# Column sums, statistics, gates, PSUM banks and weight splits in the first half of a two-layer decoder trunk on one core

## The chip, the core and the metric

The kernel runs on one NeuronCore of a Trainium2 chip. The metric is device time in microseconds (us) of one execution; the median of 3 runs of the kernel before is 1528.9 us (1528.31 to 1532.33).

## What is computed

Two layers over a sequence of 512 positions with 1024 channels, in float32. The change touches layer 0's token mixer and the part of its cross-attention that depends on the memory alone. The reference, cut to those:

```python
def rms_norm(x, g):
    y = x * lax.rsqrt(jnp.mean(x * x, axis=-1, keepdims=True) + EPS)
    return y * g

def rg_lru(x, w_gx, b_gx, w_ga, b_ga, lam):
    xh = x.reshape(Bn, S, H_A, HD_A)
    gate_x = jax.nn.sigmoid(jnp.einsum('bshi,hij->bshj', xh, w_gx).reshape(Bn, S, W) + b_gx)
    gate_a = jax.nn.sigmoid(jnp.einsum('bshi,hij->bshj', xh, w_ga).reshape(Bn, S, W) + b_ga)
    log_a = -C_RG * gate_a * jax.nn.softplus(-lam)
    a = jnp.exp(log_a)
    mult = jnp.sqrt(-jnp.expm1(2.0 * log_a))
    bx = mult * (gate_x * x)
    ...                                   # h_t = a_t * h_(t-1) + bx_t

def mixer_ab(x, norm, w_in, ...):
    z = rms_norm(x, norm) @ w_in          # 1024 -> 1024 gate | 1024 recurrent | 512 pooled
    xr = causal_dwconv(z_rec, conv_w, conv_b)
    y_a = jax.nn.gelu(z_gate) * rg_lru(xr, ...)
    y_b = multi_scale_pool(z_pool, ...)
    return jnp.concatenate([y_a, y_b], axis=-1) @ w_out

def cross_attn(x, mem, ...):
    m = rms_norm(mem, mem_norm)
    k = m @ wk                            # keys and values of 256 memory tokens
    v = m @ wv
    ...
```

After the mixer come cross-attention and a gated MLP, then layer 1 (a Conformer convolution module, cross-attention, MLP) and a final norm.

## The kernel before

Activations lie transposed, channels on the 128 partitions and the 512 positions along the free axis, so x is eight tiles `X[c]` of 128x512. Each float32 product is made of three: weights and activations are split into a high part (a ScalarE copy that rounds to the matmul format, `whi` or `act`, line 147) and a low part (a subtraction, line 148, `wlo` or `act`), and `mm3` (lines 153 to 155) multiplies high by high, high by low and low by high into one PSUM tile. The three lines appear in the profile as L153, L154 and L155. A weight piece of 128x1024 is loaded by `load_w` (lines 132 to 142) over SyncE's queue into one of three `raw` buffers; the split's products have four buffers. The subtraction of a weight piece is VectorE's, or GpSimd's where `load_w` is given `G`: in the mixer that is so for the ten pieces of `POOL_SPLITS` (line 38).

The order of the program, set at the end of `trunk` (lines 778 to 812) and then by a scheduler that places the instructions of each engine:

1. Ten products of no use at the start (line 124), while the first loads are under way.
2. Memory values of layer 0: eight pieces of `wv`, `Memory.values(0)` and `values(1)` (48 products of 512 columns each). Ahead of the first, `Memory.stats` makes the memory's norm factors.
3. The norm of x, class `Scaled`: `feed` squares each `X[c]` on ScalarE (L194), and `quarters` (L224) sums the squares over the channels on TensorE, a 32-column product in float32 for each chunk; `total` (L229) adds the four quarters. A product of float32 operands stands in the trace as two rows. Then square root (L234), reciprocal (L236), and `split` makes the normed chunk (L206) and its two parts.
4. Memory keys: eight pieces of `wk` with 24 products of 256 columns each, evicted by L303.
5. The mixer: 20 projections of 24 products each (8 `rec`, 8 `gate_branch`, 4 `pool`), four `gates` of 12 products, four `pool_map` of 3; then the output projection, 288 products.

PSUM has eight banks. Five are the pool `mm`, which all projections rotate through; two are `aux`, one is `stat`. A bank can be written again when its last reader is done: for a recurrent chunk the three convolution steps of VectorE (L508), for a gate the sigmoid (L522), for a gate branch the gelu (L544), for a pooled group the subtraction behind GpSimd's additions (L557, L562, L565 to L567). In `gates`, ScalarE runs sigmoid, exp and tanh, and sqrt, in that order.

Of the kernel before, what the change touches and what calls it, by code (L numbers as in the profile page):

```python
# [15 lines left out]
P = 128  # L16
# [20 lines left out]

POOL_SPLITS = {("rec", 3), ("rec", 4), ("rec", 5), ("rec", 7), ("pool", 1), ("pool", 3)} | {("gate", c) for c in range(4)}
# [18 lines left out]
def trunk(ctx: ExitStack, tc: tile.TileContext, I: dict, out: bass.AP):  # L57
# [35 lines left out]
    def mm_ps():  # L93
        return psum.tile([P, T], F32, tag="mm", name=nm("mm"))

    def aux_ps():
        return aux.tile([P, T], F32, tag="aux", name=nm("aux"))

# [24 lines left out]
    for _ in range(10):  # L123
        PE.matmul(idle[:, :P], onesf, onesf, start=True, stop=True)
# [61 lines left out]
    class Scaled:  # L186


        def __init__(self, gain):
            self.gain, self.x, self.sqs, self.ps = gain, [None] * C, [], None  # L190

        def feed(self, c):
            sq = tmp_f()
            A.activation(sq, X[c], AF.Square)  # L194
            self.sqs.append(sq)
            if c % 4 == 3:
                if self.ps is None:
                    self.ps = stat_ps()
                quarters(self.ps, self.sqs)

        def scale(self):
            self.r = scale_of(total(self.ps, aux_ps()))
# [46 lines left out]
    class Memory:  # L249
# [59 lines left out]
        def values(self, nh, ready=()):  # L309
            ps = [mm_ps(), mm_ps()]  # L310
            for kp in range(4):
                w = ready[kp] if kp < len(ready) else self.piece(nh * 4 + kp)
                for i in range(2):
                    k = 2 * kp + i
                    for kc in range(2):
                        mm3(ps[kc], self.chunk(k, kc * P, P), blk(w, i * T, T), k == 0, k == C - 1)
            for kc in range(2):
                hi, lo = blk(self.v[kc], nh * T, T)
                r = Memory.rt[:, kc : kc + 1]
                A.activation(hi, ps[kc], AF.Copy, scale=r)  # L320
                V.scalar_tensor_tensor(lo, ps[kc], r, hi.bitcast(F32), op0=ALU.mult, op1=ALU.subtract)
# [174 lines left out]
    def mixer(norm, nxt):  # L496
# [3 lines left out]
        def load_in(kind, c):  # L500
            at = {"gate": 0, "rec": C, "pool": 2 * C}[kind]
            return load_w(I["win"][at + c], G if (kind, c) in POOL_SPLITS else None)

# [9 lines left out]
        def gates(b, xr, xs):  # L513
# [3 lines left out]
            for i in range(2):  # L517
                c = 2 * b + i
                for g, at, bn in ((ga, T, "a_gate_a_b"), (gx, 0, "a_gate_x_b")):
                    ps = mm_ps()  # L520
                    mm3(ps, blk(gw[b // 2], at + c % 4 * P), xs[i], True, True)
                    A.activation(g[:, i * T : (i + 1) * T], ps, AF.Sigmoid, bias=col(bn, c))  # L522
            V.tensor_tensor(gx, gx, xr, op=ALU.mult)
            for i in range(2):
                at, c = slice(i * T, (i + 1) * T), 2 * b + i
                A.activation(a[:, at], ga[:, at], AF.Exp, scale=lc[:, c : c + 1])
                A.activation(ga[:, at], ga[:, at], AF.Tanh, scale=ln[:, c : c + 1])
# [6 lines left out]
            A.activation(ga, ga, AF.Sqrt)  # L534
# [70 lines left out]
        V.tensor_scalar(lc, lc, -C_RG, None, op0=ALU.mult)  # L605
        ln = small.tile([P, C], F32, tag="ln", name="ln", bufs=1)
        V.tensor_scalar(ln, lc, -1.0, None, op0=ALU.mult)
        pool(0)
# [31 lines left out]
        for j in range(C // 2):  # L640
# [7 lines left out]
            for i in range(2):  # L648
                n = 2 * j + i
                V.tensor_tensor(X[n], X[n], ps[i], op=ALU.add)  # L650
                nxt.feed(n)

# [140 lines left out]
    mem.stats()  # L793
    mem.outputs()
    mem.values(0, ready)
    for c in range(C):
        n0.feed(c)
    n0.scale()
    mem.values(1)
    for c in range(C):  # L800
        n0.split(c)
    for n in range(C):
        mem.keys(n)
    n1, n2, n3 = Norm(("xa_norm", 0)), Norm(("f_norm", 0)), Norm(("c_norm", 0))
# [75 lines left out]
```

## Time and profile before

| | us |
|---|---|
| median of 3 runs | 1528.9 (1528.31 to 1532.33) |
| profiled execution, its own time | 1529.81 |
| its span in the profile | 1528.0 |
| PE (TensorE) busy | 1496.8 |
| DVE (VectorE) busy | 926.0 |
| ACT (ScalarE) busy | 644.3 |
| POOL (GpSimd) busy | 241.4 |
| mean granted TensorE clock | 0.993 |

The span is the time from the first to the last instruction in the trace; 1.8 us of the execution's time lie around it. Busy time is the union of an engine's instructions. Products overlap in the pipeline, so two neighbours that each show 0.39 us start 0.23 us apart; the distance from start to start is the price of one. L12 is line 12 of the kernel before; PEld is the load of the stationary operand.

### The profile page before, as it was taken

Reading aid. Unit: us, or ns where it says so; the run is one execution under the profiler, and the core shown is the slowest. Engines: PE = TensorE matmul, PEld = TensorE weight load, DVE = VectorE, ACT = ScalarE, POOL = GpSimd, SP = SyncE. Lnnn points to the kernel's source line nnn. Section 1 sums busy time; section 2 is a strip of 40 time slices with the busy share of each in tenths; the row PEclk is TensorE's granted clock in tenths of the full one; section 3 lists DMA queues with packets and bytes.
Section 4 is the critical chain, followed back from the end, with each engine's and each line's share of the span. In section 5 each row is a group of like instructions: output and inputs, shape, how many; then the busy total and the mean of one; then the engine's idle time right before and its main releaser. Section 6 shows DMA issues by size and latency. Waiting matters only on the chain.

```text
span 1528.0 us, 17868 instructions
## 1 busy us (share of the span) xinstructions
PE 1496.8 (98%) x6982; PEld 1213.0 (79%) x6982; DVE 926.0 (61%) x1203; ACT 644.3 (42%) x884; POOL 241.4 (16%) x236
## 2 busy tenths in 40 slices
PE   8999999999999999999999999999999999999997
PEld 5887778888888888888877664888888888888886
DVE  6857684665655555555564996866665545555556
ACT  6566773444432323233344344644443332323223
POOL 0034410000010101010124765500001100101000
PEclk9999999999999999999999999999999999999999
DMA  7423243312333333333324543331233333333321
GB/s 254 138 87 97 83 128 101 88 56 82 93 97 98 98 109 98 107 100 99 97 84 137 165 132 103 124 97 56 69 97 97 97 97 97 97 97 97 97 83 56
DMA packets 47477, 156.24 MB, mean 102 GB/s; under 512 B 5280, under 2 KB 7328, under 8 KB 47392
## 3 DMA queue, kind: packets, MB, share of 16 engines
q1 hardware_dynamic: 46160, 154.03, 33.0%
q8 instruction: 55, 0.90, 0.2%
q10 hardware_dynamic: 1232, 1.06, 0.2%
q14 instruction: 30, 0.25, 0.0%
HBM read 144.58 MB, written 2.10 MB: 96 GB/s over the span
## 4 chain that ended last, share of the span: by engine, by line
PE 89%; DVE 4%; ACT 3%; POOL 1%; issue 1%; DMA 1%; SPq 0%; DVEq 0%; ACTq 0%; POOLq 0%
PE mm L153 28%; PE mm L154 28%; PE mm L155 28%; PE aux L700 2%; ACT whi L147 1%; DVE act L172 1%; PE stat L224 1%; PE aux L155 1%; PE aux L154 1%; POOL wlo L148 1%; PE aux L153 1%; PE aux L367 0%; DVE r L236 0%; DVE wlo L148 0%; DVE actf L763 0%
## 5 line engine op out<-in xcount | busy, mean ns | idle before, releaser
L153 PE MATMUL mm<-act,whi 128*128 128x512 f32 (+1 forms) x1908 | 740.0, 388 | 8.9 <-ACT big L522 2.7
L154 PE MATMUL mm<-act,whi 128*128 128x512 f32 (+1 forms) x1908 | 738.8, 387 | 2.7 <-DVE act L148 1.4
L155 PE MATMUL mm<-act,wlo 128*128 128x512 f32 (+1 forms) x1908 | 738.5, 387 | 0.0
L147 ACT ACTIVATE whi<-raw 128x1024 fp32r<-128x1024 f32 x267 | 282.6, 1059 | 611.4 <-PE mm L154 479.0
L153 PEld LDWEIGHTS mm<-act,whi 128*128 128x128 f32 x1908 | 360.0, 189 | 86.3 <-ACT big L522 4.7
L154 PEld LDWEIGHTS mm<-act,whi 128*128 128x128 f32 x1908 | 360.1, 189 | 78.9 <-issue 3.3
L155 PEld LDWEIGHTS mm<-act,wlo 128*128 128x128 f32 x1908 | 359.8, 189 | 74.2 <-issue 1.7
L148 DVE TENSOR_TENSOR wlo<-raw,whi 128x1024 fp32r<-128x1024 f32 x223 | 275.7, 1238 | 69.2 <-ACT whi L147 68.5
L431 POOL TENSOR_TENSOR tmp<-tmp,r 128x512 f32<-128x512 f32 x48 | 62.2, 1296 | 651.8 <-ACT tmp L430 646.9
L148 POOL TENSOR_TENSOR wlo<-raw,whi 128x1024 fp32r<-128x1024 f32 x44 | 109.0, 2480 | 159.1 <-ACT whi L147 159.1
L444 DVE TENSOR_TENSOR x<-x,mm 128x512 f32<-128x512 f32 x88 | 60.4, 687 | 99.7 <-PE mm L155 99.7
L424 DVE TENSOR_TENSOR tmp<-mm,r 128x512 f32<-128x512 f32 x48 | 33.2, 692 | 124.3 <-PE mm L155 124.2
L433 DVE TENSOR_TENSOR tmp<-mm,tmp 128x512 f32<-128x512 f32 x48 | 33.2, 691 | 95.6 <-POOL tmp L423 81.0
L718 DVE SCALAR_TENSOR_TENSOR aux<-h,par,aux 128x496 f32<-128x496 f32 (+14 forms) x105 | 75.1, 728 | 8.2 <-PE aux L700 6.0
L148 DVE TENSOR_TENSOR act<-tmp,act 128x512 fp32r<-128x512 f32 x101 | 73.7, 735 | 5.8 <-ACT act L147 5.6
L147 ACT ACTIVATE act<-tmp 128x512 fp32r<-128x512 f32 x101 | 62.9, 628 | 28.3 <-DVE tmp L180 7.6
L429 DVE SCALAR_TENSOR_TENSOR tmp<-tmp,par,tmp 128x512 f32<-128x512 f32 x96 | 71.9, 749 | 1.7
L430 ACT ACTIVATE tmp<-tmp 128x512 f32<-128x512 f32 x48 | 30.3, 632 | 95.1 <-DVE tmp L429 95.1
L423 POOL MEMSET tmp<- 128x2 f32 x48 | 4.6, 100 | 302.5 <-DVE tmp L180 302.5
L172 DVE SCALAR_TENSOR_TENSOR act<-x,par,act 128x512 fp32r<-128x512 f32 x40 | 35.6, 891 | 8.1 <-ACT act L171 8.0
L155 PE MATMUL mm<-bigr,wlo 128*128 128x256 f32 x128 | 36.3, 284 | 3.1 <-DVE wlo L148 3.1
L427 ACT ACTIVATE tmp<-tmp,par 128x512 f32<-128x512 f32 x48 | 38.6, 804 | 0.6 <-DVE tmp L424 0.6
(167 smaller groups left out, 1138.3 us busy)
## 6 DMA issues: line engine op xcount, KB each, us to landing
raw<-in_wup SPq DMA_DIRECT2D x96, 512.0 KB, 3.5
raw<-in_wdown SPq DMA_DIRECT2D x48, 512.0 KB, 3.5
raw<-in_pw SPq DMA_DIRECT2D x24, 512.0 KB, 3.6
raw<-in_win SPq DMA_DIRECT2D x20, 512.0 KB, 3.6
raw<-in_wv SPq DMA_DIRECT2D x16, 512.0 KB, 4.6
raw<-in_wk SPq DMA_DIRECT2D x16, 512.0 KB, 3.7
raw<-in_wq SPq DMA_DIRECT2D x16, 512.0 KB, 3.5
raw<-in_wo SPq DMA_DIRECT2D x16, 512.0 KB, 3.6
```

Of the source, the lines that this page charges most:

```text
L147: A.activation(hi, src, AF.Copy)
L148: (eng or V).tensor_tensor(lo, src, hi.bitcast(F32), op=ALU.subtract)
L153: PE.matmul(ps, wh, xh, start=first, stop=False)
L154: PE.matmul(ps, wh, xl, start=False, stop=False)
L155: PE.matmul(ps, wl, xh, start=False, stop=last)
L172: self.last = V.scalar_tensor_tensor(lo, X[c], g, hi.bitcast(F32), op0=ALU.mult, op1=ALU.subtract)
L424: V.tensor_tensor(g[:, 2:], ps, norm.r, op=ALU.mult)
L427: A.activation(y, g[:, 2:], AF.Identity, scale=dw(2), bias=col("f_dw_b", layer * CF + c))
L429: V.scalar_tensor_tensor(y, g[:, j : j + T], dw(j), y, op0=ALU.mult, op1=ALU.add)
L431: G.tensor_tensor(y, y, norm.r, op=ALU.mult)
L444: V.tensor_tensor(X[n], X[n], ps, op=ALU.add)
L718: V.scalar_tensor_tensor(ps[:, s:], h[:, : T - s], tap(s, c), ps[:, s:], op0=ALU.mult, op1=ALU.add)
```

## The change

- `Scaled.feed` keeps a running sum of the squares on VectorE; `scale` calls `rstd`, which splits the sum and makes two products with a matrix of ones (`mean_all`) in place of the eight 32-column products and `total`.
- `Memory.stats` is called in `values`, behind the first half's products; `n0.scale` comes behind the second half's, and the eight `n0.split` alternate with the eight `keys`.
- The gates are computed with tanh: sigmoid(z) = (1 + tanh(z/2)) / 2, with the halves folded into biases (`hb`), scales and the constant of lambda.
- `mm_ps` takes two of every seven tiles from `aux` until the mixer ends.
- The ten `POOL_SPLITS` are VectorE's.
- Fourteen products at the start in place of ten.

```diff
+    wide = [True, 0]
+
+    def mm_ps():
+
+        wide[1] += 1
+        return aux_ps() if wide[0] and wide[1] % 7 in (2, 5) else main_ps()
...
-    for _ in range(10):
+    for _ in range(14):
         PE.matmul(idle[:, :P], onesf, onesf, start=True, stop=True)
...
         def feed(self, c):
             sq = tmp_f()
             A.activation(sq, X[c], AF.Square)
-            self.sqs.append(sq)
-            if c % 4 == 3:
-                if self.ps is None:
-                    self.ps = stat_ps()
-                quarters(self.ps, self.sqs)
+            if self.ss is not None:
+                V.tensor_tensor(sq, self.ss, sq, op=ALU.add)
+            self.ss = sq

         def scale(self):
-            self.r = scale_of(total(self.ps, aux_ps()))
+            self.r = rstd(self.ss)
...
+            if Memory.rt is None:
+                self.stats()
             for kc in range(2):
                 hi, lo = blk(self.v[kc], nh * T, T)
...
-            return load_w(I["win"][at + c], G if (kind, c) in POOL_SPLITS else None)
+            return load_w(I["win"][at + c])
...
-                for g, at, bn in ((ga, T, "a_gate_a_b"), (gx, 0, "a_gate_x_b")):
+                for g, at, k in ((ga, T, C), (gx, 0, 0)):
                     ps = mm_ps()
                     mm3(ps, blk(gw[b // 2], at + c % 4 * P), xs[i], True, True)
-                    A.activation(g[:, i * T : (i + 1) * T], ps, AF.Sigmoid, bias=col(bn, c))
-            V.tensor_tensor(gx, gx, xr, op=ALU.mult)
+                    A.activation(g[:, i * T : (i + 1) * T], ps, AF.Tanh, bias=hb[:, k + c : k + c + 1], scale=0.5)
+            V.scalar_tensor_tensor(gx, gx, 1.0, xr, op0=ALU.add, op1=ALU.mult)
             for i in range(2):
                 at, c = slice(i * T, (i + 1) * T), 2 * b + i
-                A.activation(a[:, at], ga[:, at], AF.Exp, scale=lc[:, c : c + 1])
-                A.activation(ga[:, at], ga[:, at], AF.Tanh, scale=ln[:, c : c + 1])
+                l, n = lc[:, c : c + 1], ln[:, c : c + 1]
+                A.activation(a[:, at], ga[:, at], AF.Exp, scale=l, bias=l)
+                A.activation(ga[:, at], ga[:, at], AF.Tanh, scale=n, bias=n)
...
-            A.activation(ga, ga, AF.Sqrt)
+            A.activation(ga, ga, AF.Sqrt, scale=0.25)
...
-    mem.stats()
     mem.outputs()
     mem.values(0, ready)
     for c in range(C):
         n0.feed(c)
+    mem.values(1)
     n0.scale()
-    mem.values(1)
-    for c in range(C):
-        n0.split(c)
     for n in range(C):
         mem.keys(n)
+        n0.split(n)
```

The change is nine lines longer at its end, so its line numbers lie up to eleven above those of before: L153 to L155 are L158 to L160, L147 and L148 are L152 and L153, L522 is L528, L534 is L541, L544 is L551.

The scheduler's order on TensorE, at the end of the first half of the values. Before, the 32-column sums (L224) stand between the products of the second half:

```order
L153 MATMUL mm_208<-whi_253,bigr_163 128x512
L154 MATMUL mm_208<-wlo_254,bigr_163 128x512
L155 MATMUL mm_208<-whi_253,bigr_164 128x512
L224 MATMUL stat_281<-tmp_273,onesf 32x512
L153 MATMUL mm_306<-whi_310,bigr_149 128x512
L153 MATMUL mm_307<-whi_310,bigr_149 128x512
L154 MATMUL mm_306<-wlo_311,bigr_149 128x512
L155 MATMUL mm_306<-whi_310,bigr_150 128x512
L224 MATMUL stat_281<-tmp_275,onesf 32x512
```

and now the memory's statistics (L291, L216, L217) stand there, with no sums behind them:

```order
L160 MATMUL aux_190<-whi_235,bigr_168 128x512
L291 MATMUL stat_256<-onesf,big_135 128x1 x2
L216 MATMUL stat_266<-act_262,ones 128x256
L217 MATMUL stat_266<-act_263,ones 128x256
L158 MATMUL mm_300<-whi_304,bigr_153 128x512
L158 MATMUL mm_301<-whi_304,bigr_153 128x512
L159 MATMUL mm_300<-wlo_305,bigr_153 128x512
```

The eight L224 and L229 are gone from this stretch; the statistics moved behind the last product of the first half (they stood among its products before).

VectorE in the same stretch: the running sums (L201) now stand among the weight splits (L153) and the evictions of the values (L326).

```order
L326 SCALAR_TENSOR_TENSOR bigr_186<-mm_189,rt,bigr_185 128x512
L201 TENSOR_TENSOR tmp_279<-tmp_277,tmp_279 128x512
L153 TENSOR_TENSOR wlo_359<-raw_356,whi_358 128x1024
L326 SCALAR_TENSOR_TENSOR bigr_188<-aux_190,rt,bigr_187 128x512
L201 TENSOR_TENSOR tmp_282<-tmp_279,tmp_282 128x512
L153 TENSOR_TENSOR wlo_392<-raw_389,whi_391 128x1024
L201 TENSOR_TENSOR tmp_285<-tmp_282,tmp_285 128x512
L153 TENSOR_TENSOR wlo_433<-raw_430,whi_432 128x1024
```

Seven such rows are new; further on, each key's split is followed by one normed chunk (L209) where all eight chunks stood in one block before.

ScalarE in the first `gates`. Before, sigmoid (L522), exp (L526) and sqrt (L534) each have a table load ahead of them:

```order
L522 ACT_TABLE_LOAD
L522 ACTIVATE big_947<-mm_950,par 128x512
L522 ACTIVATE big_948<-mm_955,par 128x512
L147 ACTIVATE act_937<-tmp_933 128x512
L522 ACTIVATE big_947<-mm_960,par 128x512
L522 ACTIVATE big_948<-mm_965,par 128x512
L526 ACT_TABLE_LOAD
L526 ACTIVATE big_949<-big_947,lc 128x512 x2
```

and now exp follows tanh without one, and two of the four products are read from `aux`:

```order
L528 ACT_TABLE_LOAD
L528 ACTIVATE big_954<-mm_957,hb 128x512
L152 ACTIVATE act_871<-big_796 128x512
L528 ACTIVATE big_955<-aux_962,hb 128x512
L152 ACTIVATE act_944<-tmp_940 128x512
L528 ACTIVATE big_954<-mm_967,hb 128x512
L528 ACTIVATE big_955<-mm_972,hb 128x512
L533 ACTIVATE big_956<-big_954,lc 128x512 x2
```

In the third and fourth `gates` the four L528 have no table load ahead of them (they follow a gelu), and the load stands ahead of exp. From the output projection on, the engines' orders are those of before.

## Rows read from the trace of the kernel before

**Rows 1.** The page, part 1: busy time, share of the span, instructions.

```profile
PE 1496.8 (98%) x6982; PEld 1213.0 (79%) x6982; DVE 926.0 (61%) x1203; ACT 644.3 (42%) x884; POOL 241.4 (16%) x236
```

**Rows 2.** TensorE's waits, 0 to 72 us: for whom, us in total, times, longest.

```profile
PE mm L155 <- DVE wlo L148: 3.1, 1, 3.1
PE mm L154 <- DVE wlo L148: 1.6, 2, 1.0
PE stat L224 <- ACT tmp L194: 1.1, 1, 1.1
PE stat L213 <- ACT rt L290: 0.7, 1, 0.7
```

**Rows 3.** TensorE's waits, 72 to 215 us.

```profile
PE mm L153 <- ACT big L522: 2.7, 4, 0.9
PE mm L153 <- DVE big L508: 2.4, 1, 2.4
PE mm L153 <- ACT tmp L544: 2.2, 2, 2.0
PE mm L153 <- ACT tmp L557: 1.0, 1, 1.0
```

**Rows 4.** Timeline of TensorE around the mixer: start, duration, what, [idle before].

```profile
71.48 0.40 PE L153 MATMUL mm<-act,whi 128*128 128x512 f32 x1
...
122.65 0.47 PE L153 MATMUL mm<-act,whi 128*128 128x512 f32 x1 [2.35 <-DVE big L508]
...
128.16 0.63 PE L153 MATMUL mm<-act,whi 128*128 128x512 f32 x1
128.59 0.63 PE L154 MATMUL mm<-act,whi 128*128 128x512 f32 x1
...
204.44 0.50 PE L153 MATMUL mm<-act,whi 128*128 128x512 f32 x1 [0.19 <-ACT tmp L544]
...
207.39 0.50 PE L153 MATMUL mm<-act,whi 128*128 128x512 f32 x1 [1.99 <-ACT tmp L544]
...
208.68 0.63 PE L155 MATMUL mm<-act,wlo 128*128 128x512 f32 x1
...
211.24 0.63 PE L155 MATMUL mm<-act,wlo 128*128 128x512 f32 x1
```

**Rows 5.** The chain that ended last, in order of time: start, us, what.

```profile
27.23 0.97 PE stat L224 x2
28.20 0.43 PE mm L154
28.63 0.23 PE mm L155
...
33.29 0.98 PE stat L224 x4
...
40.06 0.86 PE aux L229 x2
...
279.34 0.49 PE stat L213
...
280.29 0.26 PE stat L214
```

**Rows 6.** Groups of TensorE, 0 to 72 us: the sums.

```profile
L224 PE MATMUL stat<-tmp,onesf 128*32 128x512 f32 x16 | 7.3, 604 | 1.1 <-ACT tmp L194 1.1
```

**Rows 7.** Timeline of TensorE, the first products.

```profile
1.02 4.63 PE L124 MATMUL stat<-onesf 128*128 128x128 f32 x20 [1.02 <-POOL onesf L116]
6.30 1.22 PE L153 MATMUL mm<-whi,bigr 128*128 128x512 f32 x2 [0.65 <-ACT whi L147]
...
12.86 0.50 PE L154 MATMUL mm<-wlo,bigr 128*128 128x512 f32 x1 [0.53 <-DVE wlo L148]
```

**Rows 8.** Two stretches by engine: us, PE, PEld, DVE, ACT, POOL busy, clock, DMA.

```profile
23.00:72.00 49.00, 44.09 (x261) 33.43 (x262) 39.06 (x54) 29.08 (x42) 0.11 (x1) 1.00 0.45 138
72.00:204.00 132.00, 125.94 (x539) 101.81 (x537) 83.38 (x97) 91.88 (x122) 47.03 (x28) 0.97 0.33 101
```

**Rows 9.** One line's instructions, L180: the same addition elsewhere; duration ns min/median/max.

```profile
L180 DVE TENSOR_TENSOR tmp<-tmp,tmp x35: 677/684/2478, 227.7 to 1125.0; 128x512 f32<-128x512 f32 x35
```

**Rows 10.** Groups of VectorE, 60 to 212 us: busy, mean ns.

```profile
L148 DVE TENSOR_TENSOR wlo<-raw,whi 128x1024 fp32r<-128x1024 f32 x20 | 26.4, 1323 | 8.5 <-ACT whi L147 8.4
L148 DVE TENSOR_TENSOR act<-tmp,act 128x512 fp32r<-128x512 f32 x14 | 12.6, 917 | 0.8 <-ACT act L147 0.7
```

**Rows 11.** Groups of ScalarE, 72 to 215 us: table loads ahead of exp.

```profile
L526 ACT ACT_TABLE_LOAD x4 | 5.1, 1283 | 0.1
```

More of the change, by code (lines that the diff above doesn't have):

```diff
@@ L36 @@
 WINDOWS = (2, 4, 8, 16)
-POOL_SPLITS = {("rec", 3), ("rec", 4), ("rec", 5), ("rec", 7), ("pool", 1), ("pool", 3)} | {("gate", c) for c in range(4)}
 _PARAMS = [
@@ L91, in tmp_f, with main_ps @@
         return tmp.tile([P, n], F32, tag="tmp", name=nm("tmp"))
-    def mm_ps():
+    def main_ps():
         return psum.tile([P, T], F32, tag="mm", name=nm("mm"))
@@ L189, in __init__ @@
         def __init__(self, gain):
-            self.gain, self.x, self.sqs, self.ps = gain, [None] * C, [], None
+            self.gain, self.x, self.ss = gain, [None] * C, None
         def feed(self, c):
@@ L604, in mixer @@
         V.scalar_tensor_tensor(lc, acc, 2.0, nl, op0=ALU.mult, op1=ALU.add)
-        V.tensor_scalar(lc, lc, -C_RG, None, op0=ALU.mult)
+        V.tensor_scalar(lc, lc, -C_RG / 2, None, op0=ALU.mult)
         ln = small.tile([P, C], F32, tag="ln", name="ln", bufs=1)
         V.tensor_scalar(ln, lc, -1.0, None, op0=ALU.mult)
+        hb = small.tile([P, 2 * C], F32, tag="hb", name="hb", bufs=1)
+        at = _COL["a_gate_x_b"]
+        V.tensor_scalar(hb, par[:, at : at + 2 * C], 0.5, None, op0=ALU.mult)
         pool(0)
@@ L651, in mixer @@
                 nxt.feed(n)
+        wide[0] = False
     def conformer(norm, nxt, mem):
```

## The prediction

> **What bounds the kernel now.** I first read the busy times: TensorE is busy for 1496.8 of 1528.0 us [rows 1], so no edit on another engine counts except by what it takes off TensorE, as work or as a wait. Then I asked for TensorE's waits in the two stretches that the diff touches. In the opening (0 to 72 us) four kinds of wait make 3.1 + 1.6 + 1.1 + 0.7 = 6.5 us [rows 2]; in the mixer (72 to 215 us) four more make 2.7 + 2.4 + 2.2 + 1.0 = 8.3 us [rows 3]. The timeline shows what a wait brings after it: the products behind the 2.35 us wait start 0.43 us apart instead of 0.23 (128.16 to 128.59 [rows 4]), which is TensorE at the lower of its two clock levels, 1.2 instead of 2.4 GHz. Last I read the chain that ended last, and it runs through the 32-column sums: 0.97 us for one, and 0.43 instead of 0.23 us for the product behind it [rows 5]. So the change can take at most the waits, the half clock that follows them, and the sums: about 30 us, 2%. Everything from the output projection on keeps its order and its time.
>
> **The sum, part by part.** It is made against the profiled execution's 1529.8 us, which lies 0.9 us above the median of the runs, 1528.9.
>
> *Sums to VectorE.* Sixteen rows of L224 [rows 6] are eight products of two rows. They stand in seven slots, since one slot holds two products side by side in 0.98 us [rows 5]. Seven slots of 0.97 make 6.8 us; the slower product behind each, 0.20 us, makes 1.4; `total` takes 0.86 [rows 5]. Removed: 9.1 us. Added: two products with the matrix of ones, 0.49 + 0.26 = 0.75 us by the pair at 279 us [rows 5]. Net **-8.3 us** on the engine that sets the end. The eight products have 32 columns each. The Trainium skill ("TensorE: Matmul & The Clock Gate", Packing small matmuls) says that narrow products which write different column strips run side by side, up to four, which speaks against this edit: eight would then fill two slots, and only 1.9 us plus their tails would be there to win. The trace agrees for the one slot that holds two; the other six hold one each, because the squares arrive one by one. By the two-slot count the edit would be worth 2 x 0.97 + 2 x 0.20 + 0.86 - 0.75 = 2.5 us; I take 8.3, because the rows show seven slots filled.
>
> VectorE gets seven additions of 0.68 us [rows 9] and one split of the sum (0.7 us, as a 128x512 addition): 5.5 us. It was busy for 39.1 of the 49 us from 23 to 72 [rows 8], so it has 44.6 us to do, while TensorE's stretch shrinks to about 36. The excess of some 8 us runs beside the first three projections of the mixer, 72 products of 0.23, or 16.6 us; the order has these take the normed chunks as they come. This is the tightest place of the change. If VectorE has no cover left there, the last normed chunk comes late.
>
> *Statistics behind products, chunks among keys.* The waits of rows 2 fall away one by one. The 0.7 us (L213 behind the table load and square root) goes because the statistics come after the first half's last product; but what follows them is now late instead: ScalarE's queue has the copy of the next weight piece behind the square root, so TensorE waits there for one copy and then for its subtraction. From ScalarE's and VectorE's order I put 0.7 and 0.8 us. The 1.1 and 1.0 us around the first sum go with the sums. The 3.1 us at 57 us (a key's weight split behind a block of normed chunks on VectorE) goes because chunks and keys alternate; in its place the two new products with ones wait about 0.5 us for the split sum. The last chunks for the first projection cost about 1 us. So of 6.5 us some 3.0 stay: **-3.5 us**. Bounds: nothing gained (all waits replaced by equals), 6.5 us gained. The products behind a wait start late by about 0.1 us; five fewer, -0.5.
>
> *Four more products at the start.* Four of 4.63/10 = 0.46 us, 1.9 us [rows 7]; they end at about 7.5 us where the first real product started at 6.30 [rows 7]. Twelve products later TensorE waited for a weight split until 12.86 us [rows 7] and will again, a little earlier, as the squares of the statistics no longer stand ahead of that copy. I cost this at **0**; without that cover it is 1.2 us.
>
> *Seven banks and tanh.* All four waits of rows 3 are for a bank whose reader is late: ScalarE's sigmoid behind a table load (2.7), VectorE's convolution behind the scans (2.4), the gelu behind the square root's load (2.2), the pooled copy (1.0). With seven tiles in rotation each product meets a bank two projections older, 2 x 24 x 0.23 = 11 us more slack for a projection, 1.4 us for two tiles of `gates`; and the exps of the four `gates` lose 4 loads of 1.28 us [rows 11] on the queue that frees the banks. Going through the orders by hand with the durations of before I find every bank of the mixer free at least 1 us ahead of its product. Gains: 8.3 us of waits; about 20 products at half clock in the two places (12 around 128 us and 8 from 208.68 to 211.67 us, 0.43 apart [rows 4]) x 0.20 = 4.0 us; the late starts of eight products, 0.16 each, 1.3. I keep 3.0 us for new waits at the places where the slack is about 1 us. **-10.6 us**. Bounds: 0 (the readers stay late) to -13.6.
>
> *Splits leave GpSimd.* Ten subtractions of 1.2 us go to VectorE, 12 us more in a stretch where it was busy for 83.4 of 132 [rows 8]. A part comes back: the splits of 14 activations there took 0.92 us on average and 20 of weights 1.32 [rows 10], against 0.68 for an addition of the same size that is undisturbed [rows 9], which I read as VectorE being held while GpSimd works: 14 x 0.24 = 3.4 us at least. With the stretch at about 124 us the load is 92 of 124, so I cost it at **0** on the path. What hides it is that weight splits run up to four pieces ahead; if they fall back to just in time, each late one costs a wait.
>
> Sum: -8.3 - 3.5 - 0.5 - 10.6 = -22.9, and the first half of the values ends about 1 us sooner, since statistics no longer stand in front of its weight copies: -23.9. 1529.8 - 23.9 = 1505.9, by the median 0.9 less: **1505 us**. This case's own range is 1499 to 1510.
>
> **The rivals.**
>
> *VectorE paces the opening.* For it: 44.6 us of work for 36 us of products, and the reciprocal of the norm stands in the middle of its queue. Against: the first three projections give 16.6 us of cover. If the cover is half used up by waits on ScalarE, the last chunk is some 6 us late: 1505 + 6 = 1511 us. Chance 0.18.
>
> *More banks do not help.* The reader, not the number of banks, is late: the gelu is in line behind other ScalarE work, and a bank more only moves the wait to the next product. For it: all waits of rows 3 name a reader. Against: none lasts over 2.4 us, less than half a projection. Then the mixer keeps its 10.6 us: about 1516 us. Chance 0.08.
>
> *Weight splits behind VectorE's queue: slower than before.* The ten splits now stand in VectorE's queue behind steps that wait for ScalarE's square root and behind the scans. If a split ends after TensorE has reached its piece, TensorE waits, and rows 4 show the price: 2.4 us and then 12 products at half clock, 2.4 us more, 4.8 together. The gain of 23.9 us is used up by five such events of the ten, and with eight the time is 1505 + 38 = 1543 us. It decides from the point where VectorE's work per projection passes 5.5 us; against it, 92 of 124 us is 4.1. Chance 0.04.
>
> *The sums were cheaper than their slots.* If products beside the narrow ones had used the same time, removing them gives 2.5 instead of 8.3 us: 1511 us. The chain with its 0.97 us slots speaks against it. Chance 0.03. This is what the skill's rule on narrow products would make of it.
>
> *No change that can be measured.* The scheduler moves the waits and the sum of all is small: 1529. Chance 0.03.
>
> **How the numbers follow.** Forecast 0.64, the rivals 0.18, 0.08, 0.04, 0.03, 0.03. The runs of this kernel spread by 0.26%, so about 0.3%, 4.6 us, is what a measurement can tell from no change. Faster by over 0.3% are the forecast, the first two rivals and the fourth: 0.93. Within 0.3%: 0.03. Slower: 0.04. The range takes in the forecast's own range, the first rival and the mixer's bound of 0: 1498 to 1517.
>
> **What would show it.** Right: no L224 before 870 us; the mixer's first product at 57 to 59 us instead of 71.5 [rows 4]; the output projection's first at 180 to 185 instead of 204.4 [rows 4]; waits of TensorE before 215 us of about 6 us together; the granted clock at 1.00 from 12 us to the end of the mixer. Wrong: waits of the first projections for `act` L153 (VectorE paces the opening), waits for `wlo` L153 in the mixer with the clock falling behind them (VectorE's queue), or waits for L528, L551 and L513 as large as those for L522, L544 and L508 now (banks).

## The result and the profile after

The changed kernel takes 1505.4 us (median of 4 runs, 1502.6 to 1505.7) against 1528.6 for the kernel before: a ratio of 0.984, interval 0.982 to 0.986, so 23.2 us or 1.6% faster. The forecast was 1505 (1498 to 1517). The profiled execution's span is 1503.9 us against 1528.0.

Page, part 1 of the changed kernel (engine, busy us, share, instructions), which answers to [rows 1]:

```profile
PE 1481.5 (99%) x6974; PEld 1210.1 (80%) x6974; DVE 936.2 (62%) x1222; ACT 636.5 (42%) x878; POOL 216.6 (14%) x226
```

TensorE lost 15.3 us of busy time and, in a span 24.1 us shorter, 8.8 us of idle time. To place this, one needs marks that are the same work in both kernels: the mixer's first product, the output projection's first, and its 30th, the 570th from the mixer's first. Timeline of TensorE in the changed kernel (start, duration, what):

```profile
58.49 0.40 PE L158 MATMUL mm<-act,whi 128*128 128x512 f32 x1
...
183.14 0.39 PE L158 MATMUL mm<-act,whi 128*128 128x512 f32 x1
...
189.72 0.39 PE L160 MATMUL aux<-act,wlo 128*128 128x512 f32 x1
```

The kernel before has the first two at 71.48 and 204.44 [rows 4], and the third here:

```profile
215.03 0.39 PE L155 MATMUL mm<-act,wlo 128*128 128x512 f32 x1
```

So the opening became 71.48 - 58.49 = 13.0 us shorter, and the stretch from the mixer's first product to the 30th of the output projection went from 143.6 to 131.2 us, 12.3 shorter. That is 25.3; 1.2 us are lost again behind it, where the orders are the same (no run says to what, and runs of one kernel differ by more).

TensorE's waits in the changed kernel from 0 to 58 us (for whom, us in total, times, longest), against [rows 2]:

```profile
PE mm L158 <- ACT whi L152: 1.6, 3, 0.7
PE mm L159 <- DVE wlo L153: 1.6, 3, 0.5
...
PE stat L216 <- ACT act L152: 1.0, 1, 1.0
PE stat L216 <- ACT rt L293: 0.4, 1, 0.4
```

and from 58 to 185 us, against [rows 3]:

```profile
PE mm L160 <- DVE wlo L153: 1.6, 2, 1.0
```

The 3.1 us wait of a key's split and the wait for a square are gone; a wait for the split sum (L216, 1.0 us) is new. In the mixer all four waits for banks are gone, and two waits for a weight's low part, which is VectorE's now, have come. The two stretches by engine (us, then PE, PEld, DVE, ACT, POOL busy, granted clock, DMA), against [rows 8]:

```profile
23.00:58.00 35.00, 33.86 (x236) 31.64 (x237) 33.71 (x43) 23.84 (x34) 0.00 (x0) 1.00 0.58 181
58.00:183.00 125.00, 123.43 (x546) 101.59 (x545) 96.36 (x121) 92.00 (x124) 23.43 (x20) 1.00 0.35 110
```

VectorE is busy for 33.7 of the 35 us from 23 to 58, and yet no product of the first projections waits for a normed chunk: the waits from 58 us on name only `wlo`. The mixer's granted clock is 1.00 instead of 0.97.

### The profile page after: what moved, and what is told of

Same layout as the page of the kernel before. It is cut to its first block, busy times and chain, and to the rows that moved or that the text cites. A ratio compares the mean times of both kernels' runs of the same rounds, so it can differ in the third digit from the quotient of the medians.

```text
span 1503.9 us, 17839 instructions
## 1 busy us (share of the span) xinstructions
PE 1481.5 (99%) x6974; PEld 1210.1 (80%) x6974; DVE 936.2 (62%) x1222; ACT 636.5 (42%) x878; POOL 216.6 (14%) x226
## 4 chain that ended last, share of the span: by engine, by line
PE 89%; DVE 5%; issue 2%; ACT 2%; POOL 1%; DMA 1%; SPq 0%; DVEq 0%; POOLq 0%; ACTq 0%
PE mm L159 27%; PE mm L158 27%; PE mm L160 27%; PE aux L711 2%; PE aux L160 1%; PE aux L159 1%; PE aux L158 1%; DVE wlo L153 1%; ACT whi L152 1%; DVE act L177 1%; POOL tmp L569 1%; PE aux L372 0%; DVE r L239 0%; DVE actf L774 0%; PE aux L227 0%
## 5 line engine op out<-in xcount | busy, mean ns | idle before, releaser
L159 PE MATMUL mm<-act,whi 128*128 128x512 f32 (+1 forms) x1845 | 712.8, 387 | 3.1 <-DVE act L153 1.9
L160 PE MATMUL mm<-act,wlo 128*128 128x512 f32 (+1 forms) x1845 | 712.5, 386 | 1.6 <-DVE wlo L153 1.6
L158 PE MATMUL mm<-act,whi 128*128 128x512 f32 (+1 forms) x1845 | 712.4, 387 | 0.7 <-ACT act L176 0.5
L152 ACT ACTIVATE whi<-raw 128x1024 fp32r<-128x1024 f32 x267 | 282.7, 1060 | 617.0 <-PE mm L159 460.8
L159 PEld LDWEIGHTS mm<-act,whi 128*128 128x128 f32 x1845 | 347.4, 188 | 77.0 <-issue 3.3
L160 PEld LDWEIGHTS mm<-act,wlo 128*128 128x128 f32 x1845 | 347.3, 188 | 73.7 <-DVE wlo L153 2.4
L158 PEld LDWEIGHTS mm<-act,whi 128*128 128x128 f32 x1845 | 347.5, 188 | 72.0 <-ACT act L176 1.0
L153 DVE TENSOR_TENSOR wlo<-raw,whi 128x1024 fp32r<-128x1024 f32 x233 | 288.0, 1238 | 60.5 <-ACT whi L152 60.0
L153 POOL TENSOR_TENSOR wlo<-raw,whi 128x1024 fp32r<-128x1024 f32 x34 | 82.8, 2435 | 114.4 <-ACT whi L152 114.4
L153 DVE TENSOR_TENSOR act<-tmp,act 128x512 fp32r<-128x512 f32 x102 | 73.3, 723 | 5.9 <-ACT act L152 5.7
L152 ACT ACTIVATE act<-tmp 128x512 fp32r<-128x512 f32 x102 | 63.8, 628 | 26.4 <-DVE tmp L185 7.6
L177 DVE SCALAR_TENSOR_TENSOR act<-x,par,act 128x512 fp32r<-128x512 f32 x40 | 40.2, 1008 | 8.0 <-ACT act L176 8.0
L239 DVE RECIPROCAL r<-tmp 128x512 f32<-128x512 f32 (+1 forms) x10 | 28.7, 2872 | 15.5 <-ACT tmp L237 15.5
```

Of the source, the lines that this page charges most:

```text
L152: A.activation(hi, src, AF.Copy)
L153: (eng or V).tensor_tensor(lo, src, hi.bitcast(F32), op=ALU.subtract)
L158: PE.matmul(ps, wh, xh, start=first, stop=False)
L159: PE.matmul(ps, wh, xl, start=False, stop=False)
L160: PE.matmul(ps, wl, xh, start=False, stop=last)
L177: self.last = V.scalar_tensor_tensor(lo, X[c], g, hi.bitcast(F32), op0=ALU.mult, op1=ALU.subtract)
```

## The experiments

The kernels of one submission ran on one chip beside the kernel before. Since the edits are worth 1 to 10 us and runs of one kernel differ by 3 us and more, the marks in the traces decide, and the times confirm. "Opening" is the mixer's first product, "mixer" the time from there to the output projection's 30th.

Runs of different submissions ran on different chips, where the kernel before took 1528.6 to 1531.9 us, so across them the ratios are compared and not the medians; a difference of two ratios times 1529 us is given as "by the ratios". A mark is of one execution: the profiled one of e5 is its slowest (1509.1 us, the other three 1506.6 to 1507.2), those of e1, e2, e4 and e9 are their fastest, 1.4 to 3.1 us below the median. In e6, e8, e10 and e12 nothing of the opening is edited, and their mixers begin at 57.9 to 58.3 us beside the changed kernel's 58.5, so 0.6 us is spread.

| run | median us | ratio to before, interval | opening | mixer |
|---|---|---|---|---|
| before | 1528.6 | | 71.5 | 143.6 |
| changed | 1505.4 | 0.984 (0.982 to 0.986) | 58.5 | 131.2 |
| e1 sums on TensorE | 1512.5 | 0.988 (0.986 to 0.990) | 65.0 | 132.0 |
| e2 six sums in a row | 1509.1 | 0.985 (0.983 to 0.987) | 61.4 | 131.8 |
| e3 chunks in one block | 1514.6 | 0.989 (0.987 to 0.991) | 67.5 | 131.7 |
| e4 ten idle products | 1504.5 | 0.982 (0.980 to 0.984) | 57.9 | 131.2 |
| e5 five banks | 1507.0 | 0.985 (0.983 to 0.987) | 58.0 | 135.8 |
| e6 sigmoid | 1508.4 | 0.986 (0.984 to 0.988) | 58.3 | 132.8 |
| e7 both | 1514.2 | 0.989 (0.987 to 0.991) | 57.8 | 141.2 |
| e8 splits on GpSimd | 1510.0 | 0.987 (0.985 to 0.988) | 57.9 | 135.7 |
| e9 before, sums in groups | 1523.3 | 0.995 (0.993 to 0.997) | 68.1 | 142.6 |
| e10 changed, layer norm in groups | 1503.1 | 0.982 (0.979 to 0.984) | 58.3 | 131.2 |
| e11 e10, opening's sums in groups | 1504.8 | 0.983 (0.981 to 0.985) | 60.9 | 131.9 |
| e12 e10, one key kept back | 1499.2 | 0.980 (0.978 to 0.981) | 58.3 | 131.2 |

### What the sums cost: e1, e2

e1 puts the sums back (`...` marks lines left out):

```diff
...
         def feed(self, c):
             sq = tmp_f()
             A.activation(sq, X[c], AF.Square)
-            if self.ss is not None:
-                V.tensor_tensor(sq, self.ss, sq, op=ALU.add)
-            self.ss = sq
+            self.sqs.append(sq)
+            if c % 4 == 3:
+                if self.ps is None:
+                    self.ps = stat_ps()
+                quarters(self.ps, self.sqs)
...
         def scale(self):
-            self.r = rstd(self.ss)
+            self.r = scale_of(total(self.ps, aux_ps()))
```

> The changed kernel with one part undone: the column sums of the norm go back to TensorE (eight 32-column products and the total), VectorE makes no running sum. The changed kernel took 1505.4 us. My theory (each sum that stands alone among other products costs a slot of its own): eight slots here, as they are spread in this order, less one shared pair, so 7 x 0.97 + 7 x 0.20 + 0.86 - 0.75 = 8.3 us more, 1513.7, and 0.97 us for each L229 in TensorE's chain. Rival 1 (neighbours run beside the narrow products): 2.5 us more, 1507.9. Rival 2 (the opening's gain is the order and VectorE's seven additions cost what the sums cost): under 1 us more, 1506. A wait for a square (1.1 us before) may come on top in each case.

e2 is the same with both calls of `quarters` in `scale`, so that they come late:

```diff
...
         def scale(self):
-            self.r = rstd(self.ss)
+            ps = stat_ps()
+            quarters(ps, self.sqs[:4])
+            quarters(ps, self.sqs)
+            self.r = scale_of(total(ps, aux_ps()))
```

> As e1_sums_pe, the sums on TensorE, but asked for late, so that two of the eight 32-column products stand alone and six stand directly behind each other (column strips 2, 3 and then 0 to 3). It measures what a narrow product costs with and without narrow neighbours. If narrow products on different strips run side by side up to four: the six take two slots of about 1 us, the two single ones 0.97 + 0.20 each; 2 x 1.17 + 2 x 1.0 + 0.20 + 0.86 - 0.75 = 4.7 us more than the changed kernel, 1510.1. If each takes its own slot: 8 x 0.97 + 3 x 0.20 + 0.86 - 0.75 = 8.5 us more, 1513.9. In the trace: six L228 in about 2 us, or in about 5.8 us.

A slot is the stretch that TensorE gives to a narrow product, from its start to the start of the next full product. Measured: e1's mixer begins 6.5 us later than the changed kernel's, and its time is 6.0 us longer by the ratios; the theory of slots said 8.3, the rivals 2.5 and under 1. The sums stand in seven places, as before. Two things make the difference to 8.3: with the sums on TensorE the 1.0 us wait for the split sum is not there, and e1's first half of the values happened to end 0.9 us sooner (the statistics behind it start at 19.16 against 20.07 us). e2's timeline shows a single product and the six in a row:

```profile
26.43 1.04 PE L228 MATMUL stat<-tmp,onesf 128*32 128x512 f32 x2
27.48 0.50 PE L159 MATMUL mm<-wlo,bigr 128*128 128x512 f32 x1
...
35.41 1.91 PE L228 MATMUL stat<-tmp,onesf 128*32 128x512 f32 x12
37.25 0.39 PE L158 MATMUL mm<-bigr,whi 128*128 128x256 f32 x1
```

One product (two rows) holds TensorE from 26.43 to 27.48, 1.05 us; six (twelve rows) from 35.41 to 37.25, 1.84 us, two slots. So narrow products on different column strips do run side by side when they stand together; e9 and e11 below show four in one slot. The Trainium skill says that they do ("TensorE: Matmul & The Clock Gate", Packing small matmuls), and these rows agree. Both are true at once: narrow neighbours share a slot, and the edit gained anyway, because the scheduler had put full-width products between the narrow ones. Taken together instead of taken away, the sums cost only 2.9 us of opening in e2, less than the 4.7 expected of products side by side and far from the 8.5 of a slot for each; 1.2 of it is a wait for the first square, and the wait for the split sum is gone here too.

### Where the chunks stand, and the start: e3, e4

```diff
-    mem.values(1)
     n0.scale()
+    mem.values(1)
+    for c in range(C):
+        n0.split(c)
     for n in range(C):
         mem.keys(n)
-        n0.split(n)
```

> The changed kernel with the norm's eight chunks in one block ahead of the keys (and the norm's statistics asked for ahead of the second half of the values), as the kernel before had them; sums stay on VectorE. My theory (alternating chunks and keys took away the 3.1 us wait for a key's weight split behind the chunks): that wait comes back and nothing else, 1508.5 us, with one wait of about 3 us for wlo L153 between 40 and 60 us. Rival 1 (the weights run far enough ahead, the wait had come from the sums' delays): 1505.4. Rival 2 (with the seven additions VectorE is now fuller, so the block costs more than before): wait of 5 us or more, 1510.5 or above.

e3 undoes two orders at once, the place of `n0.scale` and the alternation of chunks and keys. Together they cost 9.0 us of opening. The theory said 3.1; rival 2 (5 us or more, because VectorE is fuller now) had the direction. e3's waits from 20 to 68 us:

```profile
PE aux L158 <- DVE tmp L306: 4.6, 1, 4.6
PE mm L158 <- ACT whi L152: 1.7, 1, 1.7
```

The wait that came is not the old one (a key's weight split) but a key's eviction on VectorE, L306, which holds the bank of a later key: VectorE comes to it at 55.51 us, behind the eight chunks that it began at 46.60. The wait of 1.7 us at the start of the values' second half, 0.4 in the changed kernel, comes on top. At 56 us the clock fell too, and the 256-column products run 0.21 instead of 0.12 us apart. The window from 56 to 60 us of e3 (columns as in [rows 8]):

```profile
56.00:60.00 4.00, 3.06 (x12) 2.80 (x13) 4.00 (x7) 0.79 (x2) 0.11 (x1) 0.50 0.29 78
```

e4 takes the four products of no use away again (`range(14)` to `range(10)`).

> The changed kernel with ten products of no use at the start instead of fourteen. My prediction put the four at 0. The trace of the changed kernel shows otherwise what I had not priced: its first real products run 0.23 us apart from the start, where before eight of them ran 0.43 us apart between 8.2 and 10.7 us. Theory 0 (the wait for a weight split near 12 us hides it): 1505.4, same. Theory clock (the four keep TensorE occupied until the first real product, so that its clock is already high): the half clock of 8 products x 0.20 = 1.6 us comes back, less what the split wait covers (0.5 us), about 1 us: 1506.5. In both cases the granted clock of the first products tells.

Same time, 1504.5, and the mixer begins at 57.9 us, within the spread. The half clock is there in e4 and not in the changed kernel. Timeline of e4:

```profile
9.00 0.63 PE L158 MATMUL mm<-whi,bigr 128*128 128x512 f32 x1
9.43 0.63 PE L159 MATMUL mm<-wlo,bigr 128*128 128x512 f32 x1
```

and of the changed kernel, where two waits follow:

```profile
8.50 0.40 PE L159 MATMUL aux<-wlo,bigr 128*128 128x512 f32 x1
8.73 0.40 PE L160 MATMUL aux<-whi,bigr 128*128 128x512 f32 x1
...
10.96 0.50 PE L158 MATMUL mm<-whi,bigr 128*128 128x512 f32 x1 [0.45 <-ACT whi L152]
...
12.22 0.50 PE L159 MATMUL mm<-wlo,bigr 128*128 128x512 f32 x1 [0.53 <-DVE wlo L153]
```

In e4 the same two products start at 11.56 and 12.11 us without a wait: the faster products only reach the same weights sooner. Theory 0 holds.

### The mixer's three parts: e5 to e8

e5 sets `wide = [False, 0]`; e6 brings the sigmoid gates back (activation, biases, scales and the constant of lambda as before); e7 does both; e8 gives the ten pieces of `POOL_SPLITS` to GpSimd again:

```diff
-            return load_w(I["win"][at + c])
+            return load_w(I["win"][at + c], G if (kind, c) in POOL_SPLITS else None)
```

> The changed kernel with the mixer's products back in five banks, tanh gates kept. The stretch to watch runs from the mixer's first product to the 30th of the output projection: 143.6 us before, 131.2 us in the changed kernel. Theory (the banks bring the most, since each of the four waits was for a reader that came late by under one projection): the waits for VectorE's convolution (2.4 us), for the gelu (2.2) and for the pooled copy (1.0) and the half clock behind them (4.0) come back, the sigmoid's (2.7) do not: about 9 us, 1514. Rival 1 (table loads in the gates made the readers late; banks do not matter): under 1 us, 1506. Rival 2 (halves): 4 to 5 us, 1510.

> The changed kernel with the gates by sigmoid as before (a table load ahead of sigmoid and another ahead of exp in each of the four), seven banks kept. Theory (banks): ScalarE has up to 4 loads x 1.28 = 5.1 us more over 125 us, and two banks more of slack hide it: under 1 us more, 1506. Rival (the loads decide): 4 us or more, 1510, with waits for the gates' activation as large as the 2.7 us before.

> The changed kernel with both undone: five banks and sigmoid gates; only the weight splits on VectorE are left of the change in the mixer. Theory: the whole 12.3 us by which the stretch from the mixer's first product to the 30th of the output projection became shorter comes back, less the 2 us of waits for weight splits that the changed kernel has: 10 to 13 us more, 1516 to 1518. If the two parts add up, e5 and e6 together give this; if each alone hides the same waits, this is far more than their sum.

> The changed kernel with the ten weight splits back on GpSimd, banks and tanh kept. Theory (cost of moving them is 0 on the path): the two waits for VectorE's wlo, 0.7 + 1.2 us, go, and GpSimd's splits of about 2.4 us run far enough ahead of their products: 1503 to 1506. Rival (moving them was a gain of its own, since VectorE's instructions last longer beside GpSimd: 0.92 for 0.68 us and 1.32 for 1.22 us): 2 us or more slower, 1508.

Measured in the mixer, against the changed kernel's 131.2 us: +4.5, +1.5, +10.0 and +4.4 us; by the ratios +1.4, +2.8, +8.0 and +4.4, so that e5's mark is rather too high. TensorE's waits from 58 us to the output projection, in e5:

```profile
PE mm L158 <- DVE big L513: 1.9, 1, 1.9
PE mm L158 <- ACT tmp L551: 1.7, 1, 1.7
PE mm L158 <- ACT big L528: 0.7, 1, 0.7
```

in e6:

```profile
PE mm L160 <- DVE wlo L153: 1.8, 1, 1.8
```

in e7:

```profile
PE mm L158 <- ACT big L528: 4.5, 4, 2.2
PE mm L158 <- ACT tmp L551: 2.1, 2, 2.0
```

With five banks waits come back at three of the four readers of before (convolution, gelu, gate); the gates' are 0.7 us with tanh (e5) against 4.5 with the table loads (e7). With seven banks and sigmoid no product waits for a bank, but ScalarE's queue runs 1.1 us later (its copy of the weight's high part starts at 147.36 instead of 146.26 us), and the wait of 0.56 us for that weight's low part becomes 1.83, with the half clock behind it. So e6 is between its theory (under 1 us) and its rival (4 or more). Starting from e7, tanh alone brings 141.2 - 135.8 = 5.4 us and seven banks alone 141.2 - 132.8 = 8.4, both together 10.0, the lower end of what e7's expectation gave, while e5 and e6 add up to 6.0: each edit hides part of what the other removes. The ratios say the same, 8.0 against 4.2. e5's expectation of 9 us had counted the banks as if tanh did nothing for the other readers.

e8 refutes what I had expected: the splits' move was worth 4.4 us, its rival's "2 us or more". e8's line numbers lie two above those of the changed kernel. Its waits:

```profile
PE mm L160 <- DVE big L515: 2.5, 1, 2.5
PE mm L160 <- ACT act L154: 1.3, 1, 1.3
```

and groups of VectorE in its mixer (busy us, mean ns):

```profile
L547 DVE TENSOR_TENSOR_SCAN big<-big,big 128x512 f32<-128x512 f32 x8 | 13.6, 1736 | 0.0
L155 DVE TENSOR_TENSOR act<-big,act 128x512 fp32r<-128x512 f32 x8 | 9.2, 1151 | 3.8 <-ACT act L154 3.7
L531 DVE SCALAR_TENSOR_TENSOR big<-big,big 128x1024 f32<-128x1024 f32 x4 | 6.0, 1512 | 1.9 <-ACT big L530 1.9
L515 DVE SCALAR_TENSOR_TENSOR big<-mm,par,big 128x511 f32<-128x511 f32 x6 | 4.4, 743 | 0.9 <-ACT big L513 0.9
```

against the same groups of the changed kernel:

```profile
L545 DVE TENSOR_TENSOR_SCAN big<-big,big 128x512 f32<-128x512 f32 x8 | 11.4, 1472 | 0.0
L153 DVE TENSOR_TENSOR act<-big,act 128x512 fp32r<-128x512 f32 x8 | 5.5, 684 | 1.8 <-ACT act L152 1.8
...
L529 DVE SCALAR_TENSOR_TENSOR big<-big,big 128x1024 f32<-128x1024 f32 x4 | 4.9, 1222 | 0.5 <-ACT big L528 0.5
L513 DVE SCALAR_TENSOR_TENSOR big<-mm,par,big 128x511 f32<-128x511 f32 x6 | 4.4, 741 | 0.0
```

Three groups that read two operands from SBUF last 18 to 68% longer by their means when GpSimd makes splits; the convolution, which reads one from PSUM, does not (743 and 741 ns). The means hide that single instructions are held and the others not. Timelines of e8 from 90 to 112 us: two scans on VectorE (one row), GpSimd's split that starts with them, and the product that waits behind:

```profile
104.64 4.45 DVE L547 TENSOR_TENSOR_SCAN big<-big,big 128x512 f32<-128x512 f32 x2
104.49 2.39 POOL L155 TENSOR_TENSOR wlo<-raw,whi 128x1024 fp32r<-128x1024 f32 x1 [1.58 <-ACT whi L154]
111.19 0.76 PE L160 MATMUL mm<-act,whi 128*128 128x512 f32 x1 [2.52 <-DVE big L515]
```

and the same two scans in the changed kernel, where GpSimd does nothing from 89 to 107 us:

```profile
101.03 2.33 DVE L545 TENSOR_TENSOR_SCAN big<-big,big 128x512 f32<-128x512 f32 x2
```

Beside the split the two scans last 2.1 us longer. The convolution's steps stand behind them in VectorE's queue, the one that frees the bank starts at 110.31 us, and TensorE waits 2.52 us for it; the half clock follows. The changed kernel has the effect too: its two scan pairs beside GpSimd's L554 last 3.4 us, its other two 2.3. The Trainium skill ("SBUF — State Buffer", Who interferes with whom) names a pair of ports that VectorE and GpSimd share, one holding it while the other waits, and names VectorE's instructions with two SBUF inputs among those concerned. The rows agree. In the sum, e8's VectorE is busy for 94.5 us of its mixer with ten splits fewer, the changed kernel's for 96.4:

```profile
58.00:187.00 129.00, 124.77 (x542) 102.07 (x541) 94.45 (x110) 91.29 (x124) 51.76 (x29) 0.99 0.34 106
```

Ten splits of 1.22 us are 12.2 us of work, and VectorE is relieved of 1.9 us.

### The sums in groups: e9 to e12

e2 shows that a narrow product's price is set by its neighbours. So one edit in `quarters` keeps the four together: the product that is ready last goes first, and the others are queued directly behind it.

```diff
-        for j in range(4):
-            n = len(xs) - 4 + j
-            PE.matmul(ps[32 * j : 32 * j + 32], onesf[:, :32], xs[n], start=n < 4, stop=n >= 4)
+        def one(j):
+            n = len(xs) - 4 + j
+            return PE.matmul(ps[32 * j : 32 * j + 32], onesf[:, :32], xs[n], start=n < 4, stop=n >= 4)
+        last = one(3)
+        with tc.issue_after(last.ins):
+            for j in range(3):
+                one(j)
```

> The kernel before, with one edit in quarters: the product for the fourth chunk is issued first and the other three directly behind it, so that the four 32-column products on four column strips stand together, in the norm at the opening and in the layer norm of the Conformer (850 to 930 us). Sums stay on TensorE. From e2 (six in a row took 1.84 us, a single one 0.97 and 0.20 behind it) a group of four costs 0.9 to 1.0 and 0.20. Theory (the price of the sums was where they stood): opening 7 slots become 2, 5 x 1.17 = 5.9 us, so that the mixer begins at about 65.6 us instead of 71.5; the layer norm's 11 become 5, 7.0 us; 1528.9 - 12.9 = 1516. Rival (the group waits for its fourth square, and the waits for it and for the layer norm's chain take the gain back): mixer at 69 or later, 1524.

e9's opening is between the two, 3.4 of 5.9 us gained; its time, 1523.3, is the rival's (1524) rather than the theory's (1516). Timeline and waits (0 to 72 us) of e9:

```profile
35.34 1.07 PE L224 MATMUL stat<-tmp,onesf 128*32 128x512 f32 x8
```

```profile
PE mm L153 <- ACT whi L147: 3.4, 2, 2.1
```

A group of four costs what one product cost, but without the slots TensorE reaches a weight's high part 2.1 us before ScalarE has made it, 1.05 us more for its low part, and eleven products (26.40 to 30.83 us) follow 0.43 to 0.59 us apart, 2.5 us over their normal price. So the slots had been cover for the weight splits. The same grouping in the changed kernel is e11 against e1, and there the mixer begins 4.1 us earlier (65.0 to 60.9).

> The changed kernel with the same edit, which here reaches the Conformer's layer norm only: sixteen 32-column products that stand in 11 places come to stand in 5. Theory: 6 x 1.17 = 7.0 us less, 1498.4. Rival (VectorE, busy 104.7 of the 120 us there, sets the pace of that stretch, and the first product of the next matrix, which waits 1.45 us for VectorE's act now, waits longer): 2 us less at most, 1503.5.

e10 gains 2.7 us of span and 3.2 by the ratios, whose intervals overlap, so the gain is not clear of noise; it is nearer to the rival's 2 than to the theory's 7.0. Its waits from 840 to 945 us:

```profile
PE mm L159 <- DVE act L153: 2.9, 1, 2.9
PE mm L158 <- ACT act L152: 1.6, 1, 1.6
```

against the changed kernel's:

```profile
PE mm L159 <- DVE act L153: 1.5, 1, 1.5
```

Of the 7.0 us, 3.0 return as waits at the first product behind the layer norm, and the half clock behind them lasts for about ten products instead of seven. The last sums start 5.6 us sooner (918.1 against 923.7 us), but VectorE's `act` that TensorE waits for only 3.5 us sooner (products at 935.91 and 939.39), and TensorE has run out of other work.

> e10 with the opening's sums on TensorE again, in two groups of four, in place of VectorE's running sum. Theory (a group costs 1.17 us, and the wait of 1.0 us for the split sum falls away): against e10 2 x 1.17 + 0.86 - 0.75 - 1.2 = 1.3 us more, mixer's first product at about 60; so the running sum is the better by little. Rival (VectorE's 5.5 us less of work in the opening bring more than that): mixer's first product at 58 or earlier. Rival 2 (the wait for the fourth square of a group comes on top, as 1.2 us before the first sum in e2): 61 or later.

e11's mixer begins at 60.9, 2.6 us after e10's, between the theory (60) and rival 2 (61), with the wait of 0.95 us for the fourth square of the second group that rival 2 named. The running sum on VectorE stays the better by the marks, by less than the 6.5 us of e1; the intervals of the times overlap.

e12 adds `KE = 4` for `KE = 5` to e10.

> e10 (the changed kernel with the narrow products of the layer norm in groups), and one key of the second layer's memory more (24 products of 256 columns, 2.8 us) kept back from the MLP to the end of the layer norm, where e10's TensorE waited 1.56 + 2.85 us for ScalarE and VectorE and then ran ten products at half clock (2.0 us). Theory (e10's gain was given back there because TensorE had run out of other work): the wait shrinks by 2.8 us and the half clock goes, 4.8 us, so 1498.3. Rival (the key's weight split on GpSimd and its eviction delay the chain by as much): 1503, no better than e10.

1499.2 us, by the ratios 6.3 below the changed kernel, whose interval (0.982 to 0.986) e12's (0.978 to 0.981) does not touch. So it beats the changed kernel; against e10 (0.979 to 0.984) it gains 3.1 by the ratios and 2.7 by the spans, and the intervals overlap. Its waits behind the layer norm, 840 to 945 us:

```profile
PE mm L159 <- DVE act L153: 2.3, 2, 2.0
```

The wait shrank from 4.4 to 2.3 us; the half clock did not go, seven products still run 0.43 apart. The gain over e10 was to be 4.8. No run has `KE = 4` without the groups, so it stays open how much of the gain needs both.

## Why the prediction was right, step by step

- **What bounds the kernel.** Right: the span shrank by what TensorE lost of slots, waits and half clock, and TensorE is busy for 99% of it.
- **Sums, -8.3 us.** Sign and slots right (e1, e2), size off: undoing it costs 6.5 us, 7.4 if e1's early first half is taken off. The 1.0 us wait for the split sum belongs to this edit; I had put 0.5 of it among the opening's waits. The weighing of the Trainium skill's rule on narrow products was half right: seven slots were filled, so 8.3 and not 2.5 stood to be won, but I didn't ask whether they could be filled better, which e2, e9 and e11 answer.
- **Statistics and chunks, -3.5 us and -0.5.** Right, as far as waits tell it; no run moves the statistics back by themselves. The waits of the opening went from 7.2 us ([rows 2] and the 0.65 of [rows 7]) to 4.6, of which 1.0 is the split sum's. The waits that I named as following ones came: 0.44 and 0.53 us for the next weight's two parts behind the statistics. e3 shows that the place of `n0.scale` and the alternation of chunks and keys are worth more than this, 9 us, once VectorE has the sums: with the old order VectorE's new load would have cost more than the 6.5 us that the sums gave. So the terms of the opening do not add: 6.5 and 9.0 are more than its 13.0.
- **First half of the values, -1.** Measured 22.47 to 20.07 (0.23 us behind the start of its last product), 2.4 us less, of which the statistics' own products and wait, about 1.4, moved behind it. In e1, e3 and e10 the same mark lies at 19.2 to 20.2 us, so the size is known to about 1 us.
- **Four more products at the start, 0.** Right, with its cover (e4).
- **Opening in all.** 13.3 us were forecast, 13.0 measured; the mixer's first product was to be at 57 to 59 and is at 58.49.
- **Seven banks and tanh, -10.6.** Mechanism right (e5 to e7), and the size depends on the splits: 10.0 us with the splits on VectorE (e7 against the changed kernel), 143.6 - 135.7 = 7.9 with them on GpSimd (before against e8). The 3.0 us kept for new waits at thin banks were not needed in the changed kernel, where no product of the mixer waits for a bank; in e8 one does, for 2.5 us.
- **Splits leave GpSimd, 0.** Wrong: 4.4 us in the changed kernel (e8), and from before to e7, where of the mixer's edits only this one is left, 143.6 - 141.2 = 2.4. I had the mechanism ([rows 10] against [rows 9]) and priced its return at 3.4 us of VectorE's time "at least", but put none of it on the path, as VectorE had room. The wait is not a matter of the room: in e8 VectorE is busy for 94.5 of 129 us, and the held scans at 104.64 us still make the bank late. So the 12.3 us divide into 10.0 and 2.4 in one order of the edits, 7.9 and 4.4 in the other, and 0 for the splits is wrong in both.
- **Rivals.** VectorE paces the opening: it is full (33.7 of 35 us), but the cover held. Splits behind VectorE's queue: the two waits of 0.56 and 1.02 us are this rival's mechanism at under half the 2.4 us it was priced with, two of ten, and the clock stayed at 1.00. Banks don't help: refuted by e7 against e6, 8.4 us; with tanh already there they are worth 4.5 by the mark (e5), 1.4 by the ratios. Sums cheaper than slots: refuted by e1.
- **The signs.** The mixer's first product, the output projection's first (183.14 us, forecast 180 to 185), the waits before 215 us (4.6 + 1.6 + 0.4 = 6.6, forecast about 6) and the granted clock (1.00 from 12 us to the mixer's end) came as named. "No L224 before 870 us" was set too late: the narrow products of the layer norm, L227 now, start at 852.9 instead of 878.6, since everything before them became shorter.
- **The sum.** -23.9 forecast, -24.1 in the profiled spans. That it agrees to 0.2 us is luck: 1.8 too much for the sums (by e1) is set against 1.7 too little for the mixer, where the splits were put at 0.

## What to carry to other kernels

Ask of every small TensorE product not only how many there are but what stands beside them: narrow products on different column strips cost one slot together and one slot each apart. Before taking work off the busiest engine, look for what its time was covering: in e9 and e10 about half of a gain came back as a wait and its half clock, and with one piece of other work moved to that place (e12) 5.4 us of span were gained over the changed kernel, of the 7.0 that the grouping alone was to bring. Ten splits given to GpSimd took only 1.9 us off VectorE here, because VectorE's own instructions were held meanwhile: compare the mean duration of VectorE's own groups beside it before counting the relief.

## What the runs showed of the hardware that was not expected

A wait's length does not say whether the clock falls behind it. Products ran 0.43 us apart behind waits of 1.45 us (changed kernel, to 939.4 us), 1.83 (e6) and 1.87 (e5, to 109.3); they did not behind 1.73 us (e5, to 187.7) and behind the 3.1 us of [rows 2], where the window of the kernel before reads a granted clock of 1.00:

```profile
56.00:60.00 4.00, 0.98 (x9) 0.78 (x7) 3.79 (x7) 2.08 (x4) 0.00 (x0) 1.00 0.00 0
```

The price of a fall was about as forecast, 7 to 12 products at 0.20 us each; whether one comes has to be read from the granted clock. The relief of VectorE by GpSimd, 1.9 us for 12.2 us of work, was the other surprise.
